# Rotary embedding on one core: the first two slabs by one load, later casts, a shared last copy

## The chip, the cores and the metric

The kernel runs on one core of a Trainium2 chip. The metric is device time in microseconds (us) of one execution. Before the change the median of three runs is 160.91 us (160.87 to 160.94).

## The reference

`x` is 16 batches of 512 positions of 1024 float32 numbers, taken as 16 heads of 64. Each head's two halves are rotated by an angle of the position:

```python
x = x.reshape(batch, seq, num_heads, head_dim)
x1, x2 = x[..., :half_dim], x[..., half_dim:]
rotated = np.concatenate([x1 * cos - x2 * sin,
                          x1 * sin + x2 * cos], axis=-1)
```

`cos` and `sin` are 512 x 32 and the same for all batches and heads. Input and output have 33.6 MB each; the two tables have 64 KB each.

## The kernel before

**Slabs.** The batches are taken two at a time, as eight slabs of 4 MB. In a slab each of the 128 partitions has eight consecutive rows of 1024 numbers, 32 KB. Two neighbouring slabs lie side by side in memory, so that a partition's 64 KB of a pair of slabs are one run of bytes (`dram`, `rows`, L67).

**Places.** Three tiles `pair0` to `pair2` of 64 KB a partition hold six slots of 32 KB. `land` (L61) says in which slot a slab lands, `home` where its bf16 copy of 16 KB lies (each slot is two such half places), `leave` (L64) from which slot it is stored. Slabs 6 and 7 land where 2 and 3 had landed. A tile `spare` of 8 KB first holds the tables as they come (`raw`), and later a half slab in bf16 (`turned_part`).

**The steps of a slab.** It is loaded by SyncE's queue (`load`, L90); cast to bf16 (`cast`, L168), mostly on ScalarE; turned in place by VectorE (`turn`, L177 to 189: two multiplications with a table, L185, one of them of the halves exchanged, into a place for the crossed product, and an addition, L188); expanded to float32 (`spread`, L174) on ScalarE; stored by SyncE's queue (`store`, L94). Slabs 0, 1, 5, 6 and 7 (those in `aside`) are turned in one piece, 2, 3 and 4 in halves.

**The tables.** VectorE clears `raw` (L111). Then cos and sin are loaded into it on ScalarE's queue, 32 rows of 2 KB each (L119). GpSimd casts them to bf16 (L151), TensorE spreads them over the partitions by eight products with a selection matrix (L159), and VectorE copies the two results from PSUM to `tab` (L164). Every `turn` needs them.

**The order** on ScalarE, VectorE and SyncE is the one written out by hand from L194 on; each engine takes its instructions in that order and waits where data or a place isn't ready. Loads: slab 0, slab 1, then pairs 2-3, 4-5 and 6-7, each pair by one DMA of 128 runs of 64 KB, while slabs 0 and 1 are 128 runs of 32 KB each. The load of 4-5 waits for `turn(0)`, which uses half a slot there for its crossed product; the load of 6-7 waits for the casts of slabs 2 and 3. All loads and stores of slabs are on one DMA queue (q1), the tables on another (q10); both use the core's 16 DMA engines. Each DMA also ends with one packet of 4 bytes per engine, which reports it complete.

The first store is held back by an added dependency (L214): it waits for `gate`, the last multiplication of `turn(3)`. The last store is two DMAs of 64 partitions each, every other one (L235).

Of the kernel before, what the change touches and what calls it, by code (L numbers as in the profile page):

```python
# [9 lines left out]
@with_exitstack  # L10
def kernel(
    ctx: ExitStack,
    tc: tile.TileContext,
    x: bass.AP,
    cos: bass.AP,
    sin: bass.AP,
    num_heads: int,
    out: bass.AP,
):
    nc = tc.nc  # L20
    P = nc.NUM_PARTITIONS

    batch, seq, dim = x.shape
    nh = num_heads
    hd = dim // nh
    half = hd // 2
    bf16 = mybir.dt.bfloat16
    f32 = mybir.dt.float32

    nb = 2  # L30
    slots = 6
    nslabs = batch // nb
    G = 2
    rpp = nb * seq // P
    W = rpp * dim
    SP = seq // rpp
    TW = rpp * half

    out_flat = out.rearrange("b s h d -> b s (h d)")

    singles = ctx.enter_context(tc.tile_pool(name="singles", bufs=1))
    psum = ctx.enter_context(tc.tile_pool(
        name="psum", bufs=1, space=bass.MemoryType.PSUM))


    def dram(t, s, k):
        return bass.AP(tensor=t.tensor,
                       offset=t.offset + s // G * (G * nb * seq * dim) + s % G * W,
                       ap=[[G * W, P], [1, k * W]])


    def view(t, offset, *dims):
        return dataclasses.replace(t, offset=t.offset + offset,
                                   ap=[t.ap[0], *[list(d) for d in dims]])


    pairs = [singles.tile([P, 2 * W], f32, tag=f"pair{i}", name="pair") for i in range(slots // 2)]
    halves = [t.bitcast(bf16) for t in pairs]


    land = (0, 1, 2, 3, 4, 5, 2, 3)  # L61
    home = {0: 0, 1: 1, 2: 2, 3: 3, 5: 9, 6: 4, 7: 6}
    aside = {0: 10, 1: 3, 5: 5, 6: 5, 7: 5}
    leave = (5, 0, 5, 1, 0, 5, 1, 4)  # L64


    def rows(t, s, r, n):  # L67
        return bass.AP(
            tensor=t.tensor,
            offset=t.offset + s // G * (G * nb * seq * dim) + s % G * W + r * dim,  # L70
            ap=[[G * W, P], [1, n * dim]])


    def wide(slot, r, n):
        return view(pairs[slot // 2], slot % 2 * W + r * dim, (1, n * dim))


    def half_place(h, r, n):
        return view(halves[h // 4], h % 4 * W + r * dim, (1, n * dim))


    def thin(s, r, n):
        if s == 4:
            return half_place(8, r, n) if r + n <= rpp // 2 else view(
                turned_part, (r - rpp // 2) * dim, (1, n * dim))
        return half_place(home[s], r, n)


    def load(s, r, n):
        return nc.sync.dma_start(out=wide(land[s], r, n), in_=rows(x, s, r, n))  # L90


    def store(s, r, n):
        return nc.sync.dma_start(out=rows(out_flat, s, r, n), in_=wide(leave[s], r, n))  # L94

    def every_other(t, i):
        (step, count), rest = t.ap[0], t.ap[1:]  # L100
        return dataclasses.replace(t, offset=t.offset + i * step,
                                   ap=[[2 * step, count // 2], *rest])


    TR = 32
    TQ = seq // TR // rpp
    TC = seq * half // TR
    spare = singles.tile([P, rpp // 2 * dim // 2], f32, tag="spare")
    turned_part = spare.bitcast(bf16)
    raw = view(spare, 0, (1, TC))  # L110
    nc.vector.memset(raw, 0.0)  # L111


    def load_tables(queue):
        for i, src in enumerate((cos, sin)):
            to = dataclasses.replace(
                raw, offset=raw.offset + i * raw.ap[0][0],
                ap=[[P // TR * raw.ap[0][0], TR], [1, TC]])
            queue.dma_start(out=to, in_=bass.AP(  # L119
                tensor=src.tensor, offset=src.offset, ap=[[TC, TR], [1, TC]]))  # L120


    load(0, 0, rpp)
    load_tables(nc.scalar)
    load(1, 0, rpp)
    load(2, 0, G * rpp)

    GP = SP // G  # L130
    GT = G // TQ
    pick = singles.tile([P, 3 * GT * P], bf16, tag="pick")
    nc.gpsimd.memset(pick, 0.0)  # L133


    def selection(g, h):
        return pick[:, (g * GT + h // TQ) * P:(g * GT + h // TQ + 1) * P]


    for g in range(3):  # L140
        for h in range(0, G, TQ):
            part = view(selection(g, h), 0, (GP, P // GP), (1, GP))
            nc.gpsimd.affine_select(  # L143
                out=part, in_=part, compare_op=mybir.AluOpType.not_equal,
                fill=-1.0 if g == 2 else 1.0,
                base=-(1 if g else 0) - h // TQ * (P // TR),
                pattern=[[0, P // GP], [-(G // TQ) * (P // TR), GP]],
                channel_multiplier=1)

    raw_b = singles.tile([P, TC], bf16, tag="raw_b")  # L150
    nc.gpsimd.tensor_copy(out=raw_b, in_=raw)  # L151

    tab = {}


    def table(h):
        acc = psum.tile([P, 2 * rpp * hd], f32, tag=f"acc{h}")
        for g, at in ((0, 0), (0, half), (2, rpp * hd), (1, rpp * hd + half)):
            nc.tensor.matmul(  # L159
                view(acc, at, (hd, rpp), (1, half)), selection(g, h),  # L160
                view(raw_b, h % TQ * TW, (half, rpp), (1, half)),
                start=True, stop=True)
        tab[h] = singles.tile([P, 2 * rpp * hd], bf16, tag=f"tab{h}", name="tab")
        nc.vector.tensor_copy(out=tab[h], in_=acc)  # L164


    def cast(s, r, n, engine=nc.scalar.copy):
        engine(out=thin(s, r, n), in_=wide(land[s], r, n))  # L168


    def spread(s):
        n = rpp // 2 if s == 4 else rpp
        for r in range(0, rpp, n):
            nc.scalar.copy(out=wide(leave[s], r, n), in_=thin(s, r, n))  # L174


    def turn(s):  # L177
        n = rpp if s in aside else rpp // 2
        for r in range(0, rpp, n):
            low = thin(s, r, n)  # L180
            flip = view(low, half, (hd, n * nh), (-half, 2), (1, half))
            crossed = (half_place(aside[s], 0, n) if s in aside
                       else turned_part if s == 2 else half_place(8, n, n))
            for out_, in_, a in ((crossed, flip, rpp * hd), (low, low, 0)):
                product = nc.vector.tensor_mul(  # L185
                    out=out_, in0=in_,
                    in1=view(tab[s % G], a + r * hd, (hd, n), (0, nh), (1, hd)))
            nc.vector.tensor_add(out=low, in0=low, in1=crossed)  # L188
        return product


    with tc.manual_schedule(engines={
            mybir.EngineType.Activation, mybir.EngineType.DVE, mybir.EngineType.SP}):
        for h in range(G):  # L194
            table(h)
        v, q = nc.vector.tensor_copy, rpp // 4
        cast(0, 0, rpp)
        turn(0)
        load(4, 0, G * rpp)
        cast(1, 0, rpp)  # L200
        turn(1)
        cast(2, 0, 3 * q)
        cast(2, 3 * q, q, v)
        turn(2)
        cast(3, 0, rpp)
        load(6, 0, G * rpp)
        cast(4, 0, 2 * q)
        cast(4, 2 * q, 2 * q, v)
        cast(5, 0, 2 * q, v)
        cast(5, 2 * q, 2 * q)  # L210
        gate = turn(3)
        spread(0)
        first = store(0, 0, rpp)
        tc.add_manual_dep(  # L214
            first.ins, gate.ins.name,
            mybir.DependencyInfo(mybir.DependencyClass.Sync,
                                 mybir.DependencyReason.DATA),
            reason="shortly ahead of the end of the loads")
        spread(1)
        store(1, 0, rpp)  # L220
        cast(6, 0, rpp)
        for s in (4, 5):
            turn(s)
        for s in (2, 3, 4):
            spread(s)
            store(s, 0, rpp)
        turn(6)
        cast(7, 0, rpp)
        turn(7)
        for s in (5, 6, 7):  # L230
            spread(s)
            if s < 7:
                store(s, 0, rpp)
        for i in (0, 1):
            nc.sync.dma_start(out=every_other(rows(out_flat, s, 0, rpp), i),  # L235
                              in_=every_other(wide(leave[s], 0, rpp), i))


# [33 lines left out]
```

## Time and profile before

One execution was profiled:

| | us |
|---|---|
| its own time | 160.88 |
| span, first to last instruction | 159.1 |
| VectorE busy | 115.8 |
| ScalarE busy | 104.5 |
| slab 0 landed (ScalarE's first cast begins) | 13.4 |
| VectorE's first turn begins | 20.4 |
| pair 2-3, pair 4-5 landed (ScalarE's casts begin) | 42.3, 61.6 |
| VectorE's last pass ends | 134.5 |
| last store issued | 141.65 |

DMA moved 67.24 MB, on the mean of the span 423 GB/s. In the profile PE, DVE, ACT, POOL and SP are TensorE, VectorE, ScalarE, GpSimd and SyncE; a q behind an engine's name is its instruction queue, where DMAs are issued and waits are spent. A DMA share of 1.00 means that the packets of all 16 engines together took as long as the stretch lasts. A row of the timeline has start, duration, engine, line, operation, and in brackets the idle time before it with what ended it.

### The profile page before, as it was taken

The numbers are of one execution on the slowest core, as the hardware profiler recorded it, in microseconds if no ns is written. First come the engines' busy times: TensorE is split into PE (matmuls) and PEld (weight loads), VectorE is DVE, ScalarE is ACT, GpSimd is POOL, SyncE is SP. The second block draws the span as 40 slices with busy tenths as digits, with TensorE's granted clock in tenths as the row PEclk, the third lists the DMA queues.
The fourth block names the chain that finished last, engine by engine and source line by source line (L and its number), as shares of the span: only waits on it lengthen the run. The fifth ranks groups of instructions, "written<-read, shape, count | busy, mean of one in ns | idle before, by whom it ended". The sixth has DMA issues, their size and how long they took to land.

```text
span 159.1 us, 169 instructions
## 1 busy us (share of the span) xinstructions
PE 1.9 (1%) x8; PEld 1.1 (1%) x8; DVE 115.8 (73%) x39; ACT 104.5 (66%) x18; POOL 2.1 (1%) x9
## 2 busy tenths in 40 slices
PE   0004000000000000000000000000000000000000
PEld 0002000000000000000000000000000000000000
DVE  1002389999999999999999999999999998000000
ACT  3006939500399705999999799999999994960000
POOL 3001000000000000000000000000000000000000
DMA  6999999799699699699799999999999999999996
GB/s 239 437 412 395 478 445 527 346 445 527 280 511 527 264 527 527 264 527 478 313 395 453 470 395 395 494 428 395 461 461 395 395 494 428 395 461 461 395 395 264
DMA packets 1984, 67.24 MB, mean 423 GB/s; under 512 B 256, under 2 KB 256, under 8 KB 320
## 3 DMA queue, kind: packets, MB, share of 16 engines
q1 hardware_dynamic: 1888, 67.11, 97.9%
q10 hardware_dynamic: 96, 0.13, 0.2%
HBM read 33.69 MB, written 33.55 MB: 423 GB/s over the span
## 4 chain that ended last, share of the span: by engine, by line
DVE 53%; DMA 26%; ACT 8%; issue 2%; SPq 1%; DVEq 0%; ACTq 0%
DVE pair L185 30%; DMA pair<-in_x_dram 26%; DVE pair L188 16%; ACT pair L174 4%; DVE spare L185 4%; ACT pair L168 3%; DVE pair L168 2%; DVE spare L168 1%; SPq L90 1%; DVEq L185 0%; DVE spare L188 0%; ACTq L174 0%; ACTq L168 0%
## 5 line engine op out<-in xcount | busy, mean ns | idle before, releaser
L168 ACT CAST pair<-pair 128x8192 bf16<-128x8192 f32 (+2 forms) x8 | 47.4, 5950 | 31.4 <-DMA pair<-in_x_dram 31.4
L185 DVE TENSOR_TENSOR pair<-pair,tab 128x8192 bf16<-128x8192 bf16 (+1 forms) x18 | 62.6, 3476 | 3.6 <-ACT pair L168 3.1
L174 ACT CAST pair<-pair 128x8192 f32<-128x8192 bf16 (+1 forms) x8 | 52.5, 6590 | 3.1 <-DVE pair L188 2.1
L188 DVE TENSOR_TENSOR pair<-pair 128x8192 bf16<-128x8192 bf16 (+1 forms) x8 | 29.0, 3625 | 0.3
L164 DVE CAST tab<-acc 128x1024 bf16<-128x1024 f32 x2 | 2.4, 1218 | 13.6 <-PE acc L159 13.6
L188 DVE TENSOR_TENSOR pair<-pair,spare 128x4096 bf16<-128x4096 bf16 x2 | 4.6, 2292 | 0.1
L185 DVE TENSOR_TENSOR spare<-pair,tab 128x4096 bf16<-128x4096 bf16 x2 | 4.6, 2287 | 0.0
L174 ACT CAST pair<-spare 128x4096 f32<-128x4096 bf16 x1 | 3.6, 3602 | 0.0
L168 DVE CAST pair<-pair 128x2048 bf16<-128x2048 f32 (+1 forms) x2 | 3.5, 1756 | 0.0
L168 ACT ACT_TABLE_LOAD x1 | 1.3, 1283 | 2.6 <-issue 2.6
L168 DVE CAST spare<-pair 128x4096 bf16<-128x4096 f32 x1 | 2.3, 2293 | 0.0
L185 DVE TENSOR_TENSOR spare<-spare,tab 128x4096 bf16<-128x4096 bf16 x1 | 2.3, 2293 | 0.0
L185 DVE TENSOR_TENSOR pair<-spare,tab 128x4096 bf16<-128x4096 bf16 x1 | 2.3, 2292 | 0.0
L188 DVE TENSOR_TENSOR spare<-spare,pair 128x4096 bf16<-128x4096 bf16 x1 | 2.3, 2292 | 0.0
L159 PE MATMUL acc<-raw_b,pick 128*128 128x256 bf16 x8 | 1.9, 415 | 14.0 <-POOL raw_b L151 14.0
L159 PEld LDWEIGHTS <-pick 128*128 128x128 bf16 x8 | 1.1, 140 | 14.2 <-issue 12.3
L111 DVE MEMSET spare<- 128x512 f32 x1 | 0.5, 485 | 0.9 <-PEq L253 0.9
L143 POOL TENSOR_SCALAR_AFFINE_SELECT pick<-pick 128x128 bf16<-128x128 bf16 x3 | 0.8, 309 | 0.1
L151 POOL CAST raw_b<-spare 128x512 bf16<-128x512 f32 x1 | 0.6, 611 | 11.3 <-DMA spare<-in_sin_dram 11.3
L133 POOL MEMSET pick<- 128x384 bf16 x1 | 0.4, 419 | 0.3 <-POOLq L253 0.3
L253 POOL MEMSET const-float32-0.0<- 128x1 f32 x1 | 0.1, 100 | 0.2 <-issue 0.2
L253 POOL MEMSET const-bfloat16-1.0<- 128x1 bf16 x1 | 0.1, 103 | 0.0
(2 smaller groups left out, 0.2 us busy)
## 6 DMA issues: line engine op xcount, KB each, us to landing
out_dram<-pair SPq DMA_DIRECT2D x7, 4096.0 KB, 14.8
pair<-in_x_dram SPq DMA_DIRECT2D x2, 4096.0 KB, 17.2
out_dram<-pair SPq DMA_DIRECT2D x2, 2048.0 KB, 13.9
spare<-in_cos_dram ACTq DMA_DIRECT2D x1, 64.0 KB, 8.0
spare<-in_sin_dram ACTq DMA_DIRECT2D x1, 64.0 KB, 11.2
pair<-in_x_dram SPq DMA_DIRECT2D x3, 27.8
```

What stands on the lines that cost most here:

```text
L90: return nc.sync.dma_start(out=wide(land[s], r, n), in_=rows(x, s, r, n))
L111: nc.vector.memset(raw, 0.0)
L133: nc.gpsimd.memset(pick, 0.0)
L143: nc.gpsimd.affine_select(out=part, in_=part, compare_op=mybir.AluOpType.not_equal, fill=-1.0 if g == 2 else 1.0, base=-(1 if g else 0) - ...
L151: nc.gpsimd.tensor_copy(out=raw_b, in_=raw)
L159: nc.tensor.matmul(view(acc, at, (hd, rpp), (1, half)), selection(g, h), view(raw_b, h % TQ * TW, (half, rpp), (1, half)), start=True, sto ...
L164: nc.vector.tensor_copy(out=tab[h], in_=acc)
L168: engine(out=thin(s, r, n), in_=wide(land[s], r, n))
L174: nc.scalar.copy(out=wide(leave[s], r, n), in_=thin(s, r, n))
L185: product = nc.vector.tensor_mul(out=out_, in0=in_, in1=view(tab[s % G], a + r * hd, (hd, n), (0, nh), (1, hd)))
L188: nc.vector.tensor_add(out=low, in0=low, in1=crossed)
L253: nc = _bacc.Bacc("TRN2", target_bir_lowering=False, num_devices=1)
```

## The change

Slabs 0 and 1 come by one DMA of 128 runs of 64 KB, and the loads of 2-3 and 4-5 are issued right behind it. `raw` is cleared by GpSimd, and ScalarE copies the tables from PSUM, ahead of its first cast. Slab 0 is cast in halves. Slabs 0 to 4 are turned in halves, with `turned_part` as the crossed place of slabs 0, 1 and half of 2, and a half place of slab 4's slot, `freed`, behind that; `aside` is gone, 5, 6 and 7 use the half place 5 as before. Slab 2's cast is ScalarE's alone; of slab 5 VectorE casts five rows of eight instead of four. `gate` is the second multiplication of the first half of slab 3, and the second half of slab 2 comes behind the casts of 4 and 5. The stores of slab 6 and 7 are both two DMAs (`twice`). Slab 7's copy to float32 is half ScalarE's, half VectorE's.

```diff
-    nc.vector.memset(raw, 0.0)
+    nc.gpsimd.memset(raw, 0.0)
...
-    load(0, 0, rpp)
+    load(0, 0, G * rpp)
     load_tables(nc.scalar)
-    load(1, 0, rpp)
-    load(2, 0, G * rpp)
+    for s in (2, 4):
+        load(s, 0, G * rpp)
...
-        nc.vector.tensor_copy(out=tab[h], in_=acc)
+        nc.scalar.copy(out=tab[h], in_=acc)
...
+    n = rpp // 2
...
-        cast(0, 0, rpp)
-        turn(0)
-        load(4, 0, G * rpp)
+        for r in (0, n):
+            cast(0, r, n)
+            turn(0, r, n, turned_part)
         cast(1, 0, rpp)
-        turn(1)
-        cast(2, 0, 3 * q)
-        cast(2, 3 * q, q, v)
-        turn(2)
-        cast(3, 0, rpp)
+        for r in (0, n):
+            turn(1, r, n, turned_part)
+        for s in (2, 3):
+            cast(s, 0, rpp)
         load(6, 0, G * rpp)
-        cast(4, 0, 2 * q)
-        cast(4, 2 * q, 2 * q, v)
-        cast(5, 0, 2 * q, v)
-        cast(5, 2 * q, 2 * q)
-        gate = turn(3)
-        spread(0)
+        turn(2, 0, n, turned_part)
+        cast(4, 0, n)
+        cast(4, n, n, v)
+        cast(5, 0, n + 1, v)
+        cast(5, n + 1, n - 1)
+        freed = half_place(8, n, n)
+        turn(2, n, n, freed)
+        gate = turn(3, 0, n, freed)
+        turn(3, n, n, freed)
+        spread(0, 0, rpp)
         first = store(0, 0, rpp)
...
-        for s in (4, 5):
-            turn(s)
-        for s in (2, 3, 4):
-            spread(s)
+        for r in (0, n):
+            turn(4, r, n, freed)
+        turn(5, 0, rpp, half_place(5, 0, rpp))
+        for s in (2, 3):
+            spread(s, 0, rpp)
             store(s, 0, rpp)
-        turn(6)
+        for r in (0, n):
+            spread(4, r, n)
+        store(4, 0, rpp)
+        turn(6, 0, rpp, half_place(5, 0, rpp))
         cast(7, 0, rpp)
-        turn(7)
-        for s in (5, 6, 7):
-            spread(s)
-            if s < 7:
-                store(s, 0, rpp)
-        for i in (0, 1):
-            nc.sync.dma_start(out=every_other(rows(out_flat, s, 0, rpp), i),
-                              in_=every_other(wide(leave[s], 0, rpp), i))
+        turn(7, 0, rpp, half_place(5, 0, rpp))
+        spread(5, 0, rpp)
+        store(5, 0, rpp)
+        spread(6, 0, rpp)
+        twice(6)
+        spread(7, 0, n)
+        spread(7, n, n, v)
+        twice(7)
```

## The prediction

> **What bounds the kernel now.** I first read the page's busy shares (its parts 1 to 3), because they say whether any engine could be the limit.
>
> ```profile
> PE 1.9 (1%) x8; PEld 1.1 (1%) x8; DVE 115.8 (73%) x39; ACT 104.5 (66%) x18; POOL 2.1 (1%) x9
> ...
> DMA  6999999799699699699799999999999999999996
> ...
> q1 hardware_dynamic: 1888, 67.11, 97.9%
> ```
>
> VectorE and ScalarE have a quarter and a third of the span free; the DMA queue has nothing free. One window over the stretch in which it moves data says so more sharply (columns: busy us and instructions of PE, PEld, DVE, ACT, POOL, then clock, DMA share, GB/s):
>
> ```profile
> 1.70:157.70 156.00, 1.87 (x8) 1.01 (x7) 115.35 (x38) 104.45 (x18) 0.96 (x3) 1.00 1.00 431
> ```
>
> DMA share 1.00 from 1.7 to 157.7 us. The profiled execution took 160.88 us (the median shown is 160.91): 1.7 before the first packet, 156.0 of packets, 1.4 to the span's end at 159.1, 1.8 around the span. The chain of waits names VectorE for 53%, but VectorE only follows the same stream; it matters where it delays a transfer. So I ask two things of the change: does it shorten the stream, and does it open a hole in it?
>
> The place where a hole can open is the turn from loads to stores. The first store waits for a multiplication of slab 3, as SyncE's own waits (us in total, times, longest) and then the timeline show:
>
> ```profile
> SPq L94 <- DVE pair L185: 23.3, 1, 23.3
> ```
>
> ```profile
> 78.22 0.35 SPq L94 DMA_DIRECT2D out_dram<-pair  x1
> ```
>
> The last load, issued at 54.56, landed 26.4 us later, at 80.9; by a window from 80.05 to 80.5 all 16 engines pass there from the last load's packets to the first store's. The issue at 78.22 came 1.9 us before that (80.1), and no engine stood idle.
>
> The second place is the tables, which VectorE needs before its first pass. Their way is in the page's DMA issues (KB, us to landing) and then in the timeline (start, us):
>
> ```profile
> spare<-in_cos_dram ACTq DMA_DIRECT2D x1, 64.0 KB, 8.0
> spare<-in_sin_dram ACTq DMA_DIRECT2D x1, 64.0 KB, 11.2
> ```
>
> ```profile
> 13.31 0.61 POOL L151 CAST raw_b<-spare 128x512 bf16<-128x512 f32 x1 [11.26 <-DMA spare<-in_sin_dram]
> 13.38 7.02 ACT L168 CAST pair<-pair 128x8192 bf16<-128x8192 f32 x1 [9.46 <-DMA pair<-in_x_dram]
> 13.97 1.87 PE L159 MATMUL acc<-raw_b,pick 128*128 128x256 bf16 x8 [13.97 <-POOL raw_b L151]
> 15.02 2.35 DVE L164 CAST tab<-acc 128x1024 bf16<-128x1024 f32 x2 [13.63 <-PE acc L159]
> ```
>
> Sin, issued at 1.99, landed at 13.2, just before slab 0 (13.3), though it is 64 KB. Why so late is in windows of one packet round each, here 5.9 to 7.2 us (columns: packets, MB, share):
>
> ```profile
> q1 hardware_dynamic: 16, 0.52, 93.3%
> q10 hardware_dynamic: 16, 0.03, 6.5%
> ```
>
> Each of 16 engines moved one 32 KB packet of x, then one packet of the tables (q10). The windows from 1.7, 3.5 and 4.7 hold 16 x packets and none of q10; the six from 5.9, 7.2, 8.5, 9.7, 11 and 12.3 hold 16 q10 packets each: cos has two and a completion per engine, and sin has the same. **The tables' pace is set by the size of the x packets.**
>
> **The change part by part.**
>
> Load of slabs 0 and 1. A 32 KB packet takes 1.21 us (window 3.5 to 4.7: 101.0% of 1.2 us, one packet an engine); a 64 KB one 2.42 (window 23 to 42.2: 100.8% of 19.2 us, 8 an engine). Eight of 2.42 for sixteen of 1.21 saves nothing. Both slabs land together, when slab 1 did: ScalarE took that up at 22.97. [...]
>
> Fewer waits for loads. The load of slabs 4 and 5 no longer waits for VectorE (it was issued at 33.8 into a queue full until 42.2): nothing. The last load waits for ScalarE's casts of 2 and 3, done at 56.4 instead of 54.5; the queue is full until 61.6: nothing.
>
> Compute begins late: does that alone cost? ScalarE casts half of slab 0 from 22.95 (3.60 us by the 4096-wide casts), and VectorE starts at 26.6 instead of 20.4. A 4096-wide pass steps 2.32 (48.08 to 50.40). Slabs 0 and 1 are 12 passes, 27.85, to 54.45; half of slab 2 is three, to 61.4. The cast of slab 4's half waits until its load has landed (61.6) and ends at 63.95; five rows of slab 5 take 2.85 (between rows of 1.22 for 2048 and 2.29 for 4096, carried on), to 66.8; the other half of slab 2 ends at 73.75. The gate is now the second product of slab 3's **first** half: two passes, 78.4. It was 78.2. So six us of late start are given back by a gate three passes (6.95) earlier in the order and a quarter cast less; there is some 0.2 us of slack, in the wait at 61.6, and none behind it.
>
> The tables. This is the term that I think decides. ScalarE now copies them, ahead of every cast in its queue: cast of 0, then all else on ScalarE and VectorE, stands behind them. q10 has the same six packets an engine, but the x packets between them are twice as long. How many pass before the first table packet is seen only for 32 KB: three, though cos was issued at 1.43, 0.7 us after the first load, which began moving 1.0 us after its own issue. If the delay is time (3 to 4 us of issue and queueing), two 64 KB packets pass; if it is a depth of packets, three; zero or one is the lower bound. I take two, since cos was taken at 5.9, and the first round now ends at 4.7 (1.7 + 2.42 + 0.57 of start-up, by the first round's 1.78 for 1.21), before that, and the second at 7.2, after it. Then cos's first packet goes at 7.2, and five more x rounds bring sin's completion to 7.2 + 4 x 2.50 + 2.42 = 19.6 (2.50 with a 2 KB packet of 0.08 beside it); engines spread over 0.5 and landing 0.3 more, as before: **sin at 20.4** instead of 13.2. With three packets: 22.8. With one: 18.0.
>
> [...]
>
> From sin on: TensorE's products end 2.7 later (13.2 to 15.84), 23.1; the first half's are there at 22.3 (15.02 was 1.9 after sin). ScalarE's copies I take at 1.1 each, between VectorE's 1.22 and 1.04 from ScalarE's slope (7.02 for 8192, 3.60 for 4096; from PSUM the trace shows none): 23.4 and 24.5. The cast of 0 begins at 24.5 instead of 22.95: 1.55 late, less 0.2 of slack: gate 79.75, store issued at 79.8. Engines run dry at 80.1. From issue to moving takes between 1.0 (first load, 0.73 to 1.7) and at most 1.9 (this store, before); I take 1.3, nearer the row that saw an empty queue. **Hole: 79.8 + 1.3 - 80.1 = 1.0 us** (0.7 to 1.6 by those ends). Everything in the stream behind it moves with it.
>
> Other edits at nothing. The memset on POOL (0.42 for its neighbour's, 0.49 on VectorE) still precedes the tables' issue by ACT; without that cover it makes cos some tenths later, inside the bounds above. The last store: behind the gate VectorE has one pass of 2.32, half a slab (6.95), slab 4 in halves (13.9) and nine 8192-wide passes at 4.45, so it ends at 143.0 (134.5 before); ScalarE's half copy (3.60, VectorE's 2.29 beside it) lets the store be issued at 146.7 instead of 141.65. The stream needs it when store 6 is through, 9.7 us (eight rounds) ahead of its end: 148.0 before, 149.0 now. That is a lead of 2.3, over the 1.9 that sufficed at the turn. Halving store 6 in two DMAs: the last store, already halved, ran at share 1.00; nothing. Stores 1 to 5 follow landings and copies whose order is unchanged.
>
> Sum: 160.88 + 0 + 1.0 = **161.9 us**.
>
> **Rivals.**
> - *Three packets ahead of cos*, as in number before; for it, all 16 engines agreed on three. Sin 22.8, gate and issue 2.4 later (82.2): hole 3.4 (3.1 to 4.0), 164.3.
> - *No wait for the tables* (the other side: not slower). If cos goes after one packet or none, sin lands by 18.0, the tables are ready at 22.1, before slab 0's load; gate 78.4, issue 78.45, 0.2 later than one that left no hole. Time 160.9. It decides at sin earlier than about 19.0. Against it: q10 was passed over at 3.5 and 4.7. Faster than that needs a shorter stream, and share 1.00 leaves none.
> - *The tail*: if VectorE runs over 1 us later than summed, the last store misses its lead: 162 to 163.
> - *A burst of eight*: if an engine drained a load's eight packets before each of q10's turns, cos would go at 22, sin land at about 41, the gate come 22 us later, and the time be 183. The one-for-one windows leave it 1 in 100. [...]
>
> **How the numbers follow.** Two packets 0.48 (161.9; own range 161.5 to 162.5), three 0.27, no wait 0.20, tail 0.04, burst 0.01. The range from 160.7 to 164.8 takes in the first three with their bounds. A measurement of this kernel tells 0.2%, about 0.3 us. Same: the no-wait case but for a little on either side, 0.19; faster 0.03; slower 0.78.
>
> **What would show it.** Sin's landing in the page's DMA issues (18 to 19 us from issue; 21 or 16 for the rivals); ScalarE's first cast at 24.5 or 22.95; SyncE's first store at 79.8; DMA share under 1 only in a window round 80 to 82. Wrong would be a hole elsewhere, in the stores above all, or a stream whose 64 KB packets are not 2.42.

## The result, and the profile after

The changed kernel takes 161.52 us (median of nine, 161.43 to 161.83), the kernel before 160.97 (nine, 160.87 to 161.41): **0.3% slower**, ratio 1.0032, 95% interval 1.0021 to 1.0042. The forecast was 161.9, in a range of 160.7 to 164.8. The profiled execution took 161.57 us with a span of 159.8, 0.69 and 0.7 more than before.

The page of the changed kernel, its DMA issues (last column: us from issue to landing):

```profile
spare<-in_cos_dram ACTq DMA_DIRECT2D x1, 64.0 KB, 11.9
spare<-in_sin_dram ACTq DMA_DIRECT2D x1, 64.0 KB, 18.7
```

The tables' way in its timeline:

```profile
20.69 0.61 POOL L154 CAST raw_b<-spare 128x512 bf16<-128x512 f32 x1 [18.18 <-DMA spare<-in_sin_dram]
21.35 1.87 PE L162 MATMUL acc<-raw_b,pick 128*128 128x256 bf16 x8 [21.35 <-POOL raw_b L154]
22.40 1.93 ACT L167 CAST tab<-acc 128x1024 bf16<-128x1024 f32 x2 [18.54 <-PE acc L162]
24.21 14.30 ACT L174 CAST pair<-pair 128x4096 bf16<-128x4096 f32 x3
...
79.74 0.35 SPq L93 DMA_DIRECT2D out_dram<-pair  x1
```

Sin, issued at 1.84, lands at 20.6 instead of 13.2. ScalarE's first cast begins at 24.21 and not at 22.98, when both slabs have landed; the row has no wait of its own, for the copies of the tables stand in front of it. The first store is issued at 79.74. The chain of waits now starts with the table, where before it had started with x:

```profile
DVE 70%; DMA 12%; ACT 6%; issue 3%; PE 1%; POOLq 0%; POOL 0%; ACTq 0%; DVEq 0%
DVE pair L185 37%; DVE pair L188 21%; DMA spare<-in_sin_dram 12%; DVE spare L185 9%; ACT pair L178 2%; ACT pair L174 2%; DVE pair L174 2%; DVE spare L174 1%; ACT tab L167 1%; PE acc L162 1%; POOLq L274 0%; POOL pick L136 0%; ACTq L122 0%; DVEq L185 0%; POOL spare L114 0%
```

Why sin is late: a window of one round of packets, 7.1 to 9.6 us (packets, MB, share):

```profile
q1 hardware_dynamic: 16, 1.05, 96.7%
q10 hardware_dynamic: 16, 0.03, 3.4%
```

As before, one packet of x and one of the tables per engine, but the former is 64 KB now (1.05 MB for 16). The windows from 1.7 and 4.7 have no table packet: two x packets go ahead of cos.

The hole, the time in which the DMA engines have nothing to move: the window from 80.05 to 80.58, in the changed kernel and then in the kernel before.

```profile
DMA packets 16, 0.00 MB, mean 0 GB/s; under 512 B 16, under 2 KB 16, under 8 KB 16
```

```profile
q1 hardware_dynamic: 32, 0.52, 230.6%
```

Before, every engine reports the load complete (16 small packets) and begins on the store (16 of 32 KB) in that half microsecond. After, there are the 16 reports and nothing else. The stores then also run slower. A round of store packets is one packet of 32 KB on each engine. Windows over 63 of the 64 rounds (last columns: DMA share, GB/s), before and after:

```profile
80.10:156.35 76.25, 0.00 (x0) 0.00 (x0) 53.87 (x16) 58.45 (x10) 0.00 (x0) 1.00 1.00 433
```

```profile
80.58:157.22 76.64, 0.00 (x0) 0.00 (x0) 64.09 (x20) 54.19 (x10) 0.00 (x0) 1.00 1.00 431
```

The same bytes take 76.64 us instead of 76.25. From the traces' packet records, as means over the 16 engines (a round is the time from the first store packet's begin to the last one's end, by 64):

| us | before | changed |
|---|---|---|
| first x packet begins | 2.01 | 1.95 |
| last x packet ends | 80.28 | 80.28 |
| first store packet begins | 80.29 | 80.64 |
| a round of store packets | 1.2103 | 1.2168 |
| last store packet ends | 157.74 | 158.52 |

So 0.36 us is the hole and 0.42 (64 x 0.0065) the slower rounds. The engines end closer together (0.16 us apart, 0.37 before), and on the last of them, which ends the run, 0.66 is left.

### The profile page after: what moved, and what is told of

It is laid out like the page before. It is cut to its first block, busy times and chain, and to the rows that moved or that the text cites. A ratio compares the mean times of both kernels' runs of the same rounds, so it can differ in the third digit from the quotient of the medians.

```text
span 159.8 us, 178 instructions
## 1 busy us (share of the span) xinstructions
PE 1.9 (1%) x8; PEld 1.1 (1%) x8; DVE 115.8 (72%) x42; ACT 104.1 (65%) x21; POOL 2.5 (2%) x10
## 4 chain that ended last, share of the span: by engine, by line
DVE 70%; DMA 12%; ACT 6%; issue 3%; PE 1%; POOLq 0%; POOL 0%; ACTq 0%; DVEq 0%
DVE pair L185 37%; DVE pair L188 21%; DMA spare<-in_sin_dram 12%; DVE spare L185 9%; ACT pair L178 2%; ACT pair L174 2%; DVE pair L174 2%; DVE spare L174 1%; ACT tab L167 1%; PE acc L162 1%; POOLq L274 0%; POOL pick L136 0%; ACTq L122 0%; DVEq L185 0%; POOL spare L114 0%
## 5 line engine op out<-in xcount | busy, mean ns | idle before, releaser
L178 ACT CAST pair<-pair 128x8192 f32<-128x8192 bf16 (+1 forms) x8 | 49.2, 6165 | 12.2 <-DVE pair L188 10.2
L185 DVE TENSOR_TENSOR pair<-pair,tab 128x4096 bf16<-128x4096 bf16 (+1 forms) x19 | 56.3, 2965 | 0.7
L174 ACT CAST pair<-pair 128x8192 bf16<-128x8192 f32 (+2 forms) x9 | 48.6, 5406 | 9.3 <-DMA pair<-in_x_dram 9.3
L185 DVE TENSOR_TENSOR spare<-pair,tab 128x4096 bf16<-128x4096 bf16 x5 | 11.5, 2292 | 28.3 <-ACT pair L174 27.9
L188 DVE TENSOR_TENSOR pair<-pair 128x4096 bf16<-128x4096 bf16 (+1 forms) x7 | 22.4, 3207 | 0.2
L167 ACT CAST tab<-acc 128x1024 bf16<-128x1024 f32 x2 | 1.9, 1015 | 18.5 <-PE acc L162 18.5
L188 DVE TENSOR_TENSOR pair<-pair,spare 128x4096 bf16<-128x4096 bf16 x5 | 11.5, 2292 | 0.2
L174 DVE CAST pair<-pair 128x5120 bf16<-128x5120 f32 x1 | 2.8, 2827 | 0.0
L178 DVE CAST pair<-pair 128x4096 f32<-128x4096 bf16 x1 | 2.3, 2294 | 0.1
L114 POOL MEMSET spare<- 128x512 f32 x1 | 0.5, 524 | 0.3 <-POOLq L260 0.3
## 6 DMA issues: line engine op xcount, KB each, us to landing
spare<-in_cos_dram ACTq DMA_DIRECT2D x1, 64.0 KB, 11.9
spare<-in_sin_dram ACTq DMA_DIRECT2D x1, 64.0 KB, 18.7
```

What stands on the lines that cost most here:

```text
L114: nc.gpsimd.memset(raw, 0.0)
L167: nc.scalar.copy(out=tab[h], in_=acc)
L178: engine(out=wide(leave[s], r, n), in_=thin(s, r, n))
L185: product = nc.vector.tensor_mul(out=out_, in0=in_, in1=view(tab[s % G], a + r * hd, (hd, n), (0, nh), (1, hd)))
```

## The experiments

Theory: the tables wait in turn behind 64 KB packets; ScalarE's casts wait for the tables; the gate and the first store follow, and the engines stand idle at the turn from loads to stores. Rivals: the late landing of the slabs itself, the larger runs, or the new order of copies and stores. "Ratio" is against the kernel before.

**The size of the runs undone.**

```diff
-    load(0, 0, G * rpp)
+    load(1, 0, rpp)
     load_tables(nc.scalar)
+    load(0, 0, rpp)
```

> The changed kernel, but slabs 1 and 0 (in that order) come by two DMAs of 32 KB runs, so that the cast of slab 0 still begins when both have landed, and only the size of the runs is undone. Theory (the tables wait in turn behind 64 KB packets, and that makes the first store late): sin lands at 13.2 as before, ScalarE's first cast begins at 22.95, first store issued at 78.4, no hole, store rounds of 1.210 us; 160.97, ratio to the kernel before 1.000 (0.999 to 1.001). Rival (the late start of compute itself costs): first cast at 22.95 as the theory says, but the time stays at 161.5. Rival (the changed stores, slab 6 in halves among them, run slower): store rounds stay at 1.217, time 161.4.

161.29 us, ratio 1.0023 (1.0010 to 1.0037). The profiled execution, of 161.08, is as the theory has it: sin at 13.2, first store issued at 78.44, no hole, rounds of 1.2105. Its timeline, and then the window from 80.02 to 80.55, in which every engine again goes from its report to a store packet:

```profile
13.34 0.61 POOL L155 CAST raw_b<-spare 128x512 bf16<-128x512 f32 x1 [10.83 <-DMA spare<-in_sin_dram]
22.94 14.29 ACT L175 CAST pair<-pair 128x4096 bf16<-128x4096 f32 x3 [5.96 <-DMA pair<-in_x_dram]
...
78.44 0.35 SPq L93 DMA_DIRECT2D out_dram<-pair  x1
```

```profile
q1 hardware_dynamic: 32, 0.52, 230.8%
```

So neither the late landing nor the new stores make the hole. But ten executions spread from 161.08 to 161.93, and the median is 0.34 us over that of before, where the changed kernel's is 0.55 over. Two more executions were profiled for that:

> The kernel with slabs 1 and 0 by two loads of 32 KB runs once more, for the cause of its scatter (161.08 to 161.93 in ten executions; the one profiled took 161.08 and had no hole). Theory: in a slower execution the first store, issued at 78.4, meets the last load packet or finds the engines free, so that either that packet is longer than 2.45 on the mean, or there is a hole and rounds of 1.217. Rival: the whole load stream is longer, and the turn is as in the other.

> The same kernel a third time, with the same two answers to tell apart.

They took 161.78 and 161.36. In both the turn is as in the first (no hole, last x packet 2.42 us, rounds of 1.210). The load stream is longer: 78.81 and 78.62 us from first to last x packet, 78.22 in the first. Some rounds of 64 KB loads took 2.44 to 2.57 instead of 2.42. A window of 19.5 us of loads in the first profile and in that of 161.78 shows it:

```profile
42.00:61.50 19.50, 0.00 (x0) 0.00 (x0) 19.17 (x9) 13.94 (x2) 0.00 (x0) 1.00 0.99 430
```

```profile
42.00:61.50 19.50, 0.00 (x0) 0.00 (x0) 19.17 (x9) 13.94 (x2) 0.00 (x0) 1.00 0.98 417
```

VectorE and ScalarE do the same in both. What slows those packets in some executions isn't settled; the kernel before has executions up to 161.7 too, of which none was profiled.

**The tables first, runs of 64 KB kept.**

```diff
+    for t in pairs:
+        nc.gpsimd.memset(view(t, 0, (1, 8)), 0.0)
+    load_tables(nc.sync)
     load(0, 0, G * rpp)
-    load_tables(nc.scalar)
```

> The changed kernel, 64 KB runs kept, but cos and sin are issued on SyncE's queue ahead of the first load, which (like the next two) waits for GpSimd's clearing so that the order holds. The tables no longer take turns with x. Theory: sin lands near 5; the x stream begins about 1.25 later (3.2 on the mean of the engines) and saves the tables' 0.34 inside, so loads end at 81.2; both slabs land at 23.9 and the first cast begins there, with no wait for the tables; first store issued at 79.4, 0.85 ahead of its packets: no hole, store rounds of 1.210; 161.9, all of the 0.9 at the start. Rival (64 KB runs or the late landing make the hole, not the tables): a hole of 0.4 and rounds of 1.217 as in the changed kernel, 162.5 or more.

162.90, ratio 1.0107 (1.0079 to 1.0135). The DMA issues and timeline of this kernel:

```profile
spare<-in_cos_dram SPq DMA_DIRECT2D x1, 64.0 KB, 2.0
spare<-in_sin_dram SPq DMA_DIRECT2D x1, 64.0 KB, 2.1
```

```profile
5.82 1.93 ACT L169 CAST tab<-acc 128x1024 bf16<-128x1024 f32 x2 [3.80 <-PE acc L164]
24.85 14.30 ACT L176 CAST pair<-pair 128x4096 bf16<-128x4096 f32 x3 [17.10 <-DMA pair<-in_x_dram]
```

With nothing of x ahead of them cos landed in 2.0 us and sin in 2.1, not in 11.9 and 18.7. The cast waits for x alone, the store is issued at 80.36, the last x packets end at 81.88 to 82.41: no hole, rounds of 1.2115. The theory holds with 64 KB runs. The time was missed by 1.0, of which 0.9 is at the start: the x stream begins at 4.09, not 3.2, two issues of some 0.6 and the wait for GpSimd ahead of it.

**More table packets, the same bytes.**

```diff
-            queue.dma_start(out=to, in_=bass.AP(
-                tensor=src.tensor, offset=src.offset, ap=[[TC, TR], [1, TC]]))
+            cut = TC // (1 + i)
+            for c in range(0, TC, cut):
+                queue.dma_start(
+                    out=dataclasses.replace(
+                        to, offset=to.offset + c, ap=[to.ap[0], [1, cut]]),
+                    in_=bass.AP(tensor=src.tensor, offset=src.offset + c,
+                                ap=[[TC, TR], [1, cut]]))
```

> The changed kernel with sin loaded by two DMAs of 1 KB rows instead of one of 2 KB: the same bytes, but nine table packets an engine instead of six. Theory (a turn behind one 64 KB packet for each table packet): sin lands 3 x 2.45 us later, at 27.9; first cast at 31.6, first store issued at 87.1, hole 7.4 longer; 168.9, ratio 1.049. Rival (the tables wait for bytes or for a fixed delay, not for turns): sin at 20.6, 161.5.

166.74, ratio 1.0361 (1.0347 to 1.0375). Sin landed at 25.4, two turns of 2.45 later and not three; the store was issued 4.86 us later, at 84.60, and the last store packets ended 4.86 later (the time rose by 5.2). The missing turn is in the window from 22.0 to 24.4:

```profile
q1 hardware_dynamic: 32, 1.05, 101.1%
q10 hardware_dynamic: 32, 0.03, 3.8%
```

Two table packets an engine passed here, and of q1's 32 packets 16 are the 4-byte reports that the first load is complete. One table packet for one of q1's, here too, and a 4-byte report took a turn of q1's as a 64 KB packet did in the windows before: in this run the turns went by packets, not by bytes.

**Smaller first packets.**

```diff
-    load(0, 0, G * rpp)
+    load(1, 0, rpp // 2)
     load_tables(nc.scalar)
+    load(1, rpp // 2, rpp // 2)
+    load(0, 0, rpp)
```

> The changed kernel with slab 1 loaded first and in two DMAs of 16 KB runs, then slab 0 in 32 KB runs; the tables are issued behind the first of them. Theory (one x packet for each table packet, whatever its size): sin lands well ahead of 13.2, at about 9 to 10 (16 KB packets take 0.6); both slabs still landed at 22.95, first cast there; first store issued at 78.4, no hole; 161.0 to 161.3, as with two loads of 32 KB runs. Rival (a time of issue and queueing that does not depend on the packets): sin at 13.

Sin landed at 9.1, as expected. 161.63, ratio 1.0036 (1.0022 to 1.0050), 0.3 over: the x stream took 78.35, and the store rounds 1.2129 with the engines drifting from 0.54 to 0.74 us apart; why isn't known. It also shows when cos comes up. Its first packet began at 5.5 behind five packets of 16 KB, at 5.9 behind three of 32 (the kernel before), at 7.3 behind two of 64 (the changed kernel), and was passed over at 4.8, 4.7 and 4.9. So cos did not wait for a fixed number of packets: it was five, three and two. As my reading of these times, a time fits, to about 5 us, and after that the packet in progress; so would a number of bytes, for each time cos was passed over with 64 KB of x moved on an engine and taken at 80 KB or more. These runs don't tell the two apart.

**The gate moved.** Three passes later, and two passes earlier (the last product of slab 2):

```diff
-        gate = turn(3, 0, n, freed)
-        turn(3, n, n, freed)
+        turn(3, 0, n, freed)
+        gate = turn(3, n, n, freed)
```

> The changed kernel with the first store waiting for the last multiplication of slab 3's second half, three passes later. Theory: issue at 86.7 instead of 79.74, the hole 6.97 longer, nothing gives it back: 168.5, ratio 1.047. Rival (the hole is made up for later, because the stores behind it have slack): between 161.5 and 166.

```diff
-        turn(2, n, n, freed)
-        gate = turn(3, 0, n, freed)
+        gate = turn(2, n, n, freed)
+        turn(3, 0, n, freed)
```

> The changed kernel with the first store waiting for the last multiplication of slab 2 instead of slab 3's first half. Theory: tables late as in the changed kernel (sin at 20.6, first cast at 24.2), but the store is issued when ScalarE's copy of slab 0 is done, at 75.3, ahead of the loads' end; no hole, store rounds 1.210, 160.97, ratio 1.000. Rival (a store queued 5 us ahead of the loads' end slows the loads, which is why it was held back): loads land later than 81.05, time over 161.2. Rival (something else in the changed kernel costs the 0.55): 161.5.

Later: 168.62, ratio 1.0474 (1.0461 to 1.0488). The issue moved by 7.19, the time by 7.10: this hole at the turn was not made up for. Earlier: 162.18, ratio 1.0071 (1.0059 to 1.0083), slower than the changed kernel; the theory's number was wrong here. The store, issued at 75.20, left no hole, and the rounds were 1.2103. But the last x packet was longer. The window from 77.4 to 80 has that packet of every engine, in the changed kernel and with the early gate:

```profile
q1 hardware_dynamic: 16, 1.05, 93.0%
```

```profile
q1 hardware_dynamic: 16, 1.05, 129.3%
```

93.0% of 2.6 us is 2.42, 129.3% is 3.36. The store that was queued this early cost the loads 0.95 us. How early is too early was asked twice, with the first product of slab 3 as the gate; in the changed kernel, and with two loads of 32 KB runs:

```diff
+        first = None
         for out_, in_, a in ((crossed, flip, rpp * hd), (low, low, 0)):
             product = nc.vector.tensor_mul(
...
+            first = first or product
         nc.vector.tensor_add(out=low, in0=low, in1=crossed)
-        return product
+        return first
```

> The changed kernel with the first store waiting for the first multiplication of slab 3, one pass (2.32 us) earlier; loads, tables and casts stay as in the changed kernel. The issue should come at 77.4, its packets be ready at 78.3: after the engines have begun their last load packet (77.7 to 78.1), before they are free (80.1). Theory of the hole, with the earlier run's finding that only the last load packet is slowed, and only by a store that is there before that packet begins: no hole, last load packet of 2.42 us, store rounds of 1.210; 160.95, ratio 1.000, though the tables still land at 20.6. Rival (the cost of an early store grows evenly with its earliness, 1.0 us at 75.2, nothing at 78.2): 161.2. Rival (the late tables cost in another place too): 161.5.

> Slabs 1 and 0 by two loads of 32 KB runs as in an earlier run, and the first store waiting for the first multiplication of slab 3. The issue comes at 76.1, packets ready at 77.0, before the last load packet begins. Theory: that packet takes 3.36 us instead of 2.42, as with the store issued at 75.2; 161.9 to 162.1. Rival (earliness costs evenly): 161.6. Rival (only a store over 4 us early costs): 161.0 to 161.3.

Issued at 77.37: 161.58, ratio 1.0041 (1.0028 to 1.0053). Issued at 76.03: 162.34, ratio 1.0083 (1.0068 to 1.0099). The last x packet took 2.80 and 3.58 on the mean. At 77.37 some engines lost 0.8 us and others nothing (their first store packets lie 1.08 us apart). My bound, that a store may come once that packet has begun, was too kind. Over all runs, an issue 1.5 to 2.0 us ahead of the first engine's end of loads cost neither the packet nor a hole; 2.7 ahead (77.37 against 80.07) was too early, 0.34 ahead (the changed kernel's 79.74 against 80.08) too late.

**The hole without the change.** The kernel before, with the gate on slab 3's last addition:

```diff
-            nc.vector.tensor_add(out=low, in0=low, in1=crossed)
+            product = nc.vector.tensor_add(out=low, in0=low, in1=crossed)
         return product
```

> The kernel before with one edit: the first store waits for slab 3's last addition, one pass (2.29 us) later. Issue at 80.53, packets from 81.4, hole 1.1 us per engine. If a hole also makes the store rounds slower, as in the changed kernel (1.217 instead of 1.210, engines 0.15 us apart instead of 0.38), 162.3, ratio 1.008. If the slower rounds belong to the changed kernel's own stores or copies, rounds stay at 1.210 and the time is 161.9, ratio 1.006.

162.37, ratio 1.0086 (1.0073 to 1.0099), with a hole of 1.19 us. Its window over 63 store rounds:

```profile
81.40:158.06 76.66, 0.00 (x0) 0.00 (x0) 52.62 (x15) 57.18 (x10) 0.00 (x0) 1.00 1.00 431
```

It is 76.25 without the late gate. So the slower rounds (1.217 for 1.210 us) came with the hole, not with the changed stores.

**The pair load alone**, in the kernel before:

```diff
-    load(0, 0, rpp)
+    load(0, 0, G * rpp)
     load_tables(nc.scalar)
-    load(1, 0, rpp)
```

> The kernel before with one edit: slabs 0 and 1 by one DMA of 64 KB runs. Nothing else of the change. Theory: first cast at 22.95, turn of slab 0 to 43.4, where the load of slabs 4 and 5 still waits for it (hole of 2.3); slab 3's cast and the last load later in the same way (hole of 1.3); the gate at 88.0 against loads that end at 84 (hole of 4.9); with slower store rounds 169.9, ratio 1.056. Rival (late landing is covered by slack in compute, and only the tables' wait matters): VectorE copies the tables by 24.7, before its first pass needs them at 30.0, so 161.0 to 162.

169.77, ratio 1.0546 (1.0531 to 1.0560). In its timeline, the load of slabs 4 and 5, late behind slab 0's turn, and the first store:

```profile
43.49 0.33 SPq L90 DMA_DIRECT2D pair<-in_x_dram  x1
...
87.90 0.35 SPq L94 DMA_DIRECT2D out_dram<-pair  x1
```

Here the late landing does cost: 8.8 us. Pair 4-5 lands 3.9 later than before (65.4), pair 6-7 another 1.2 (86.0), and the hole ahead of the store is 3.7. The rest of the change (the loads that no longer wait for VectorE, slab 0 cast in halves, the gate three passes earlier, the second half of slab 2 behind the casts) takes all but 0.55 of them back; which part takes how much was not tried.

## Why the prediction was right, and where its sizes were off

- *The bound is the DMA stream, and only a hole can move it.* Right for this change: the load streams end at 80.28 in both, and a gate later by 7 us cost 7. A store issued at 75.20 lengthened the last x packet from 2.42 to 3.36 us without a hole, which the prediction did not have.
- *64 KB runs save nothing.* Right: 2.42 a packet, for two of 1.21. Their first round took 3.13, 0.71 over a packet; with 32 KB it took 1.78, 0.57 over. The difference is gone by the end of the loads (80.28 in both).
- *The tables take turns, two x packets ahead of cos.* Right; sin at 20.6 for 20.4. The rival of three packets fell; the run with 16 KB packets rules out a fixed number of packets, and leaves a time or a number of bytes. The burst of eight fell too: 16 packets of each queue, one for one, in each of the six windows from 7.1 to 22 us.
- *First cast at 24.5, gate at 79.75, issue at 79.8.* Measured 24.21, 79.71, 79.74. That the issue agrees so well is in part luck. The cast came 0.3 earlier; ScalarE's copies took 1.02 each (1.1 assumed, 1.04 by its slope). But the 0.2 of slack was not there: against the run with 32 KB loads, the cast is 1.27 later (24.21 for 22.94) and the issue 1.30 (79.74 for 78.44).
- *The hole, 1.0 us.* This term was mis-sized: 0.36. I took 1.3 us from issue to moving; the store needed 0.85 (79.74 to 80.59), less than the first load's 1.0, my lower end. 1.9 was only a bound from a full queue. And 80.1 is when the first of the 16 engines runs dry; their mean is 80.28.
- *The rest of the stream just moves with the hole.* Wrong: behind the hole its rounds were 0.5% slower (1.2168 for 1.2103), 0.42 us, a term that the sum did not have. The two errors cancel in part: 0.66 us in the profiles and 0.55 in the medians, for 1.0. That the time still lies in the forecast's own range (161.5 to 162.5), at its lower end, is luck.
- *Late compute is covered.* Right for the whole change: the last store was issued at 146.75 (146.7), and the stream behind it was full. With its first part alone the cover is gone (169.77).
- *No wait for the tables gives 160.9.* Half shown: 161.08 in one profile and 161.29 in the median, with the load stream's scatter between. No version tried beats the kernel before.

## What to carry to other kernels

Here a small transfer on a second queue waited by packets, not by bytes (sin, 64 KB, landed at 13.2 between packets of 32 KB, at 20.6 between packets of 64 KB, and at 25.4 with nine packets an engine instead of six): before making the main stream's packets larger, count the small one's packets, completions included, and multiply by the new packet time. Where this stream turned from loads to stores, the first store had a window of issue: 1.5 to 2.0 us ahead of the loads' end was right, 2.7 slowed the last loads (2.80 us a packet for 2.42), 0.34 left a hole of 0.36, and both went into the time (what lies between was not tried). A step that starts six microseconds later cost little here only because what frees the next transfer was moved ahead with it.

## What the runs showed of the hardware

- After all 16 engines had run dry, they went on in step, their packets 0.14 to 0.15 us apart, and a round of store packets took 1.2168 to 1.2170 in all five such kernels (the changed one, the later gate, the split sin, the late store and the pair load alone). The nine profiles without such a hole have them 0.38 to 1.08 apart and 1.2103 to 1.2129. That the closeness makes it is a guess that was not tried by itself; it does not order the other nine (1.2129 at 0.54 apart, 1.2103 at 0.38).
- A store queued early came with a longer last load packet: 3.36 us (issued at 75.20), 3.58 (76.03), 2.80 (77.37) on the mean of the engines, for 2.42; issued at 78.22 it left it at 2.43. The mechanism is open.
- With loads of x issued around it, the first engine passed cos over 3.6 us after its issue (at 4.9, the changed kernel), and took it 4.2 us after (at 5.5, the 16 KB packets), 4.5 (at 5.9, the kernel before) and 6.0 (at 7.3, the changed kernel); all of it had landed 2.0 us after issue when it was first. What it waited for is open.
